# HGRN2 chunk scores in blocks of 64 tokens instead of 32, with a seventh masked level

## The chip, the cores and the metric

The kernel runs on one core of a Trainium2 chip. The metric is device time in microseconds (us) for one execution: the median of three executions is 2924.04 us (2918.29 to 2924.26).

## What is computed

The reference is one inference step of a decoder of two layers. Every layer projects 2064 prompt tokens (16 learned tokens and 2048 of the prompt) and 8 sample tokens by one combined matrix. Four mixers work on the columns of the product: HGRN2, gated DeltaNet, Mamba-2 SSD and retention, with four heads of 64 channels each. One output projection closes the layer. The change is inside HGRN2, whose decay is a vector: each key channel has its own decay at each token.

```python
def chunk_vector_decay(S, xs):
    q, k, v, g = xs
    G = jnp.cumsum(g, axis=2)
    causal = jnp.tril(jnp.ones((c, c), bool))
    diff = G[:, :, :, None, :] - G[:, :, None, :, :]
    decay = masked_exp(diff, causal[:, :, None])
    scores = jnp.einsum('bhik,bhjk,bhijk->bhij', q, k, decay)
    o = (jnp.einsum('bhij,bhjv->bhiv', scores, v)
         + jnp.einsum('bhik,bhkv->bhiv', q * jnp.exp(G), S))
    ...
```

A score of query i with key j needs the product of the decays between j and i in every channel, so the scores of a chunk are not one plain matrix product.

## The kernel before

The prompt is cut into a first tile (32 token rows for the 16 learned tokens and padding, with the 8 samples behind them) and 16 chunks of 128 tokens. Eight blocks of two chunks each (the first block has the small tile too) are the unit of the dense projections. A layer runs its mixers in turn: SSD (mixC), the dense part of gated DeltaNet (denseB and prepB), HGRN2 (mixA), retention (mixD), then the output projection. The serial walk over the gated DeltaNet states (walkB) is emitted in small parts, by hook(), among the work of the other mixers, above all in mixA. Dense products are made in three exact parts (lines 473 to 475 and 483 to 485) of 256 columns each.

mixA (from line 701) takes a block: dense products for q, f (the decay), kk, v and z, and then, for a group of two chunks (in the first block also a group of the small tile alone), the scores by levels. Level 0 (mask hm0) takes the diagonal: products of q and kk as they are. Then q is multiplied by its own token's decay and the loop at line 766 runs over h = 1, 2, 4, ... 64. At level h a pair counts if key and query lie in the left and right half of the same stretch of 2h tokens. Behind each level's products, right halves of q are multiplied by the left half's whole decay and left halves of kk by the right half's (lines 778 to 783), so that at the next level a plain product of q and kk is the decayed score again.

For levels 0 and h = 1 to 16 scores(32, 0) (line 736) multiplies blocks of 32 keys by the 32 queries of the same tokens: for a chunk 4 blocks x 2 pairs of heads x 2 heads of a pair = 16 products, each on 64 rows (a head's channels) and 32 columns of the TensorE array; the two heads lie in the two halves of the rows, the four blocks in the four quarters of the columns. merge (line 751) brings the level into the tile sm (`aS`, 128 x 256 for a group): level 0 by multiplying with its mask, the others by a predicated copy under the level's mask. At h = 32 and 64 scores(h, h) multiplies only the left half's keys by the right half's queries, and ScalarE copies the result directly into the chunk's full triangle (s128, tile `sq`; line 773). At the end GpSimd copies sm's four diagonal blocks into the triangle, eight copies a chunk (lines 804 to 807), and four products with v make the output (line 809).

All scores go through one PSUM buffer of two banks, pair() (line 199, one buffer). sm comes from w1 (tag W1, four buffers of 1 KB a partition, also used by `low` and `akt`); the running decay products aT come from w2 (tag W2, four buffers of 2 KB, also used by prepB for bR, bdc and others; line 215). Inputs are 32-bit floats, and each product of lines 745, 795 and so on shows in the trace as two matmul records, each with a weight load.

The order of instructions on each engine is not written out: a planner (the scheduler of the tile framework, line 1773) lays out a simulated timeline by priority and free buffers when the kernel is built, and each engine then runs its list in that order. What is emitted inside early() goes ahead in priority; inorder() fixes the order on chosen engines.

Of the kernel before, what the change touches and what calls it, by code (L numbers as in the profile page):

```python
# [33 lines left out]
def make_consts(nch):  # L34
    f = np.float32
# [22 lines left out]
    for n, h in enumerate((0, 1, 2, 4, 8, 16)):  # L58
        j = (p % 32)[:, None]
        if h == 0:  # L60
            parts[f"hm{n}"] = j == i32
        else:
            parts[f"hm{n}"] = (j // (2 * h) == i32 // (2 * h)) & (j % (2 * h) < h) & (i32 % (2 * h) >= h)
# [29 lines left out]
def body(tc, ctx, a, o, nch, depth, blks, off):  # L93
# [105 lines left out]
    def pair():  # L199
        """a bank per head half: row tiles of the array may not share a bank"""  # L200
# [44 lines left out]
    # ---------------------------------------------------------------- constants  # L245
# [15 lines left out]
    def fill():  # L261
# [6 lines left out]
        tt(strict, C("u32c"), C("hm0"), ALU.subtract)  # L268
# [5 lines left out]
    # block-diagonal states (two heads a tile), in turns  # L274
# [4 lines left out]
    # full triangles (upper halves written), in turns; outside of their use: norm weights, retention's decay  # L279
# [8 lines left out]
    def next_state(L, m, pu, decay):  # L288
        """S = decay * S + update, block-diagonal"""
# [25 lines left out]
    # ---------------------------------------------------------------- helpers  # L315
# [4 lines left out]
    def power(dst, src, k=0):  # L320
        """src ** -0.5 (k=0) or 0.5 (k=1)"""
# [23 lines left out]
    def rms_scale(hx, R):  # L345
        """1 / rms of the rows"""
# [6 lines left out]
    # ---------------------------------------------------------------- per layer parameters  # L353
    def load_layer(l):
# [38 lines left out]
        # forget gate bounds: softmax of the logits over the depth axis, cumulative  # L393
# [34 lines left out]
    # ---------------------------------------------------------------- dense pieces  # L428
# [66 lines left out]
    def xprep(L, t, hx, keep=False):  # L495
        """normalised rows of a token tile -> channel-major, in two exact parts, to DRAM or to the block's tiles"""
# [32 lines left out]
    def rowtile(b, nm):  # L529
        """token-major rows of 256 columns by tile"""  # L530
# [6 lines left out]
    def small(L, b, raw):  # L537
        """decays and step sizes from the narrow columns of a block's tiles"""
# [31 lines left out]
        # cumulative sums: ssd over the chunk, gdn over blocks of 32  # L570
# [15 lines left out]
    def group_scale(osrc, R, groups, eps):  # L586
        """rows scaled by 1 / rms of each group, in SBUF; eps: number or [R, groups]"""
# [26 lines left out]
    def finish(t, mi, osrc, R, eps, w, z, b=None):  # L614
        """group norm of the mixer rows; returns what takes them to channel-major, gate z [128, 2, R], and to DRAM"""
# [27 lines left out]
    # decode: partitions hold (head half, key), free (sample, pair, value)  # L643
# [12 lines left out]
    def dec_bcast(rows8):  # L656
        """[8, 256] rows -> [128 (hh k), (b p), 64]"""
# [8 lines left out]
    def pb(x, cols=None):  # L666
        """[128, 2, 8] channel-major sample columns -> [128, 8, 2, 64] broadcast over values"""
# [8 lines left out]
    def dec_sum(src, lhs, m):  # L676
        """sum over the key partitions"""
# [18 lines left out]
    # ---------------------------------------------------------------- HGRN2  # L696
# [4 lines left out]
    def mixA(L, W, b):  # L701
# [26 lines left out]
        for c0, Lc, tl in groups:  # L728
# [1057 lines left out]
```

## Time and profile before

| | |
|---|---|
| median of three executions | 2924.04 us (2918.29 to 2924.26) |
| span of the profiled execution | 2924.2 us |
| TensorE matmul busy | 2811.0 us (96%) |
| TensorE weight load busy | 2631.0 us (90%) |
| VectorE / ScalarE / GpSimd busy | 58% / 35% / 36% |
| HGRN2 stage with the walk beside it, layer 1 and layer 2 | about 650 to 1010 us, 2090 to 2500 us |

The span of the profiled execution lies within the three times, so nothing to speak of lies around it. PE is the matmul side of TensorE, PEld its weight loads, DVE is VectorE, ACT ScalarE, POOL GpSimd, SP the engine that issues most DMAs. Matmuls are pipelined: a record's duration is longer than the distance to the next record's start, so what a burst of matmuls costs is read from its first start to the start of what follows. Some records are missing from a trace.

### The profile page before, as it was taken

What the parts mean: (1) busy time and instruction counts of PE and PEld (TensorE: products, weight loads), DVE (VectorE), ACT (ScalarE), POOL (GpSimd) and SP (SyncE); (2) the same over time, 40 slices, a digit from 0 to 9 for tenths busy, and PEclk for the clock granted to TensorE, in tenths of its full rate; (3) what the DMA queues carried; (4) which work ended last, traced back from release to release, by engine and by line L of the source; (5) the groups of instructions that cost most, each with busy time, mean ns of one, the idle gap of its engine ahead of it and who ended that gap; (6) DMA issues with size and microseconds to landing.
All of it is one profiled execution on the core that took longest, in us unless ns stands there. A gap on an engine that the chain in (4) does not pass through costs nothing.

```text
span 2924.2 us, 76217 instructions
## 1 busy us (share of the span) xinstructions
PE 2811.0 (96%) x31196; PEld 2631.0 (90%) x31196; DVE 1694.9 (58%) x4822; ACT 1010.7 (35%) x2547; POOL 1045.4 (36%) x2000
## 2 busy tenths in 40 slices
PE   6989999999999999999999999899999999999998
PEld 6889898988888899999999999888988888999998
DVE  6777765646566745364456767565556657445433
ACT  5545522333333412232244454133333333222221
POOL 4453555665232211110033543745742222112000
PEclk9999999999999999999999999999999999999999
DMA  7243364462231432247762433645432222331433
GB/s 181 68 151 118 127 163 122 133 188 76 63 112 60 129 95 88 74 128 212 215 204 93 127 106 103 152 128 152 139 101 69 78 99 83 96 116 63 134 131 109
DMA packets 391332, 349.92 MB, mean 120 GB/s; under 512 B 144312, under 2 KB 361904, under 8 KB 380744
## 3 DMA queue, kind: packets, MB, share of 16 engines
q1 hardware_dynamic: 387464, 335.96, 37.5%
q0 software_dynamic: 3520, 9.09, 1.5%
q8 instruction: 247, 4.05, 0.6%
q14 instruction: 101, 0.83, 0.1%
HBM read 247.06 MB, written 98.10 MB: 118 GB/s over the span
## 4 chain that ended last, share of the span: by engine, by line
PE 84%; DVE 6%; DMA 4%; POOL 3%; ACT 2%; issue 2%; SPq 0%; POOLq 0%; ACTq 0%; DVEq 0%
PE pd L473 10%; PE pd L474 10%; PE pd L483 10%; PE pd L484 10%; PE pd L475 10%; PE pd L485 10%; PE tr L235 7%; PE sc L235 5%; PE wo L235 5%; PE o L235 3%; DMA wr<-in_w_in_dram 1%; PE tr L611 1%; PE tr L507 1%; DVE hx L502 1%; POOL bR L1110 1%
## 5 line engine op out<-in xcount | busy, mean ns | idle before, releaser
L473 PE MATMUL pd<-xh,wh 128*128 128x256 f32 (+1 forms) x2816 | 832.1, 296 | 12.6 <-DVE hB L901 3.3
L474 PE MATMUL pd<-xl,wh 128*128 128x256 f32 (+1 forms) x2816 | 817.9, 290 | 0.0
L475 PE MATMUL pd<-xh,wl 128*128 128x256 f32 (+1 forms) x2816 | 814.1, 289 | 0.0
L483 PE MATMUL pd<-wh,xh 128*128 128x256 f32 (+3 forms) x2448 | 702.0, 287 | 6.4 <-DVE sraw L1342 4.6
L484 PE MATMUL pd<-wl,xh 128*128 128x256 f32 (+3 forms) x2448 | 700.8, 286 | 2.5 <-POOL wl L450 2.5
L485 PE MATMUL pd<-wh,xl 128*128 128x256 f32 (+3 forms) x2448 | 698.0, 285 | 0.2
L473 PEld LDWEIGHTS pd<-xh,wh 128*128 128x128 f32 x2816 | 543.9, 193 | 37.2 <-issue 16.8
L474 PEld LDWEIGHTS pd<-xl,wh 128*128 128x128 f32 x2816 | 543.8, 193 | 9.1 <-issue 6.6
L475 PEld LDWEIGHTS pd<-xh,wl 128*128 128x128 f32 x2816 | 543.6, 193 | 4.1 <-issue 2.6
L483 PEld LDWEIGHTS pd<-wh,xh 128*128 128x128 f32 (+1 forms) x2448 | 455.7, 186 | 12.6 <-issue 5.4
L484 PEld LDWEIGHTS pd<-wl,xh 128*128 128x128 f32 (+1 forms) x2448 | 455.8, 186 | 9.0 <-issue 3.4
L485 PEld LDWEIGHTS pd<-wh,xl 128*128 128x128 f32 (+1 forms) x2448 | 455.7, 186 | 4.4 <-issue 2.1
L304 DVE TENSOR_TENSOR sbd<-low,tr 64x128 f32<-64x128 f32 x384 | 109.0, 284 | 131.8 <-PE tr L235 113.4
L600 POOL TENSOR_SCALAR fm<-fm 128x4 f32<-128x4 f32 (+3 forms) x102 | 23.7, 233 | 419.2 <-DVE fm L597 393.1
L1613 DVE TENSOR_TENSOR hx<-hx,pd 128x256 f32<-128x256 f32 (+1 forms) x136 | 57.1, 420 | 175.5 <-PE pd L485 175.2
L327 POOL TENSOR_TENSOR fm<-fm,expo 128x4 f32<-128x4 f32 (+3 forms) x136 | 129.3, 951 | 49.0 <-DVE fm L602 38.7
L331 POOL TENSOR_SCALAR rm<-rm 128x1 f32<-128x1 f32 (+1 forms) x51 | 13.7, 269 | 367.2 <-ACT junk L349 366.3
L520 ACT ACTIVATE th<-pd 128x256 f32<-128x256 f32 (+2 forms) x162 | 62.3, 384 | 231.8 <-PE pd L475 194.9
L235 PEld LDWEIGHTS sc<-aq,ak 64*32 64x32 f32 (+1 forms) x7008 | 97.0, 108 | 39.7 <-issue 16.9
L235 PE MATMUL sc<-aq,ak 64*32 64x32 f32 (+1 forms) x7008 | 129.1, 200 | 2.5 <-ACT sq L773 2.0
L1110 POOL TENSOR_TENSOR bR<-bR,bW 128x120 f32<-128x120 f32 (+14 forms) x300 | 119.6, 399 | 21.6
L1109 POOL TENSOR_TENSOR bW<-bU,bR 128x120 f32<-128x120 f32 (+14 forms) x300 | 112.6, 375 | 36.4 <-DMA bR<-bscr 15.4
(519 smaller groups left out, 4989.0 us busy)
## 6 DMA issues: line engine op xcount, KB each, us to landing
xh<-xh SPq DMA_DIRECT2D x56, 1024.0 KB
xl<-xl SPq DMA_DIRECT2D x56, 1024.0 KB
wr<-in_w_in_dram SPq DMA_DIRECT2D x64, 512.0 KB
hx<-in_x_prompt_dram SPq DMA_DIRECT2D x32, 512.0 KB
y<-y SPq DMA_DIRECT2D x128, 128.0 KB
yf<-y SPq DMA_DIRECT2D x32, 512.0 KB
bld<-qkv SPq DMA_DIRECT2D x32, 384.0 KB
xh<-xh SPq DMA_DIRECT2D x8, 1184.0 KB
```

The source lines that it names most:

```text
L235: T.matmul(out, l, r, start=start, stop=stop, skip_group_check=True)
L304: tt(new[rr, :, hh], low[rr, :, hh], pv, ALU.add)
L327: G.tensor_tensor(dst, src, e.broadcast_to(list(src.shape)), ALU.pow)
L473: T.matmul(ps, hi[:, d], b.xh[:, d, 0:b.n], start=(d == 0), stop=False)
L474: T.matmul(ps, hi[:, d], b.xl[:, d, 0:b.n], start=False, stop=False)
L475: T.matmul(ps, lo[:, d], b.xh[:, d, 0:b.n], start=False, stop=(d == 7))
L483: T.matmul(ps[0:R, 0:n], xh[:, d], hi, start=(d == 0), stop=False)
L484: T.matmul(ps[0:R, 0:n], xh[:, d], lo, start=False, stop=False)
L485: T.matmul(ps[0:R, 0:n], xl[:, d], hi, start=False, stop=(d == 7))
L520: act(th[0:R, 0:n], ps, AF.Tanh, scale=0.5)
L1109: f(wv, bcm(U_[0:2 * nu, j, j + 1:32], 1, m), bcl(R_[0:2 * nu, 0:m, j], 31 - j), ALU.mult)
L1110: f(R_[0:2 * nu, 0:m, j + 1:32], R_[0:2 * nu, 0:m, j + 1:32], wv, ALU.subtract)
```

## The change

The blocks on which a level's products are made become 64 keys by 64 queries (H = 64; 32 for the small tile): for a chunk 2 blocks x 2 x 2 = 8 products, each on 64 rows and 64 columns of the array, so that the two heads and the two blocks fill its four quarters. h = 32 becomes a level like the others (mask hm6, `copy_predicated`) and no longer goes through ScalarE; h = 64 stays (across()). The loop over the blocks stands inside the one over the head pairs. sm doubles to 128 x 512 for a group and moves from w1 to w2. GpSimd copies two diagonal blocks of 64 a chunk, four copies instead of eight. The masks hm0 to hm6 are 64 columns wide, and a separate identity e32 takes the place of hm0 where gated DeltaNet used it; the constant table grows from 756 to 1044 columns. The other lines of the diff take out comments.

```diff
-    for n, h in enumerate((0, 1, 2, 4, 8, 16)):
-        j = (p % 32)[:, None]
+    i64 = np.arange(64)
+    for n, h in enumerate((0, 1, 2, 4, 8, 16, 32)):
+        j = (p % 64)[:, None]
...
+    parts["e32"] = (p % 32)[:, None] == i32
...
-            def scores(h, w):
-                pv = pair()[:, :, 0:ncn * 2 * h].rearrange("j x (c p i) -> j x c p i", c=ncn, p=2)
+            H = min(64, Lc)
+
+            def scores():
+                pv = pair()[:, :, 0:ncn * 2 * H].rearrange("j x (c p i) -> j x c p i", c=ncn, p=2)
                 for c in range(ncn):
-                    for j0 in range(0, Lc, h + w):
-                        cc = c0 + Lc * c + j0
-                        for p in range(2):
+                    for p in range(2):
+                        for j0 in range(0, Lc, H):
+                            cc = c0 + Lc * c + j0
                             for hh in range(2):
                                 rr = slice(64 * hh, 64 * hh + 64)
-                                mm(pv[j0:j0 + h, hh, c, p], kk[rr, p, cc:cc + h], q[rr, p, cc + w:cc + w + h],
+                                mm(pv[j0:j0 + H, hh, c, p], kk[rr, p, cc:cc + H], q[rr, p, cc:cc + H],
                                    start=(c == 0 and p == 0), stop=True)
                 return pv
+            def across():
+                pv = pair()[:, :, 0:ncn * 2 * 64].rearrange("j x (c p i) -> j x c p i", c=ncn, p=2)
...
+                            mm(pv[0:64, hh, c, p], kk[rr, p, cc:cc + 64], q[rr, p, cc + 64:cc + 128],
+                               start=(c == 0 and p == 0), stop=True)
...
-            sm = w1([128, 2, 2, 2, 32], "aS")
+            sm = w2([128, 2, 2 * ncn, H], "aS")
...
-                if h < 32:
-                    merge(k, scores(32, 0))
+                if h < 64:
+                    merge(k, scores())
                 else:
-                    pv = scores(h, h)
+                    pv = across()
                     for c in range(ncn):
-                        for j0 in range(0, 128, 2 * h):
-                            S.copy(s128[(L.tai + c) % 2][j0:j0 + h, :, j0 + h:j0 + 2 * h].rearrange(
-                                "j (p x) i -> j x p i", p=2), pv[j0:j0 + h, :, c])
+                        S.copy(s128[(L.tai + c) % 2][0:64, :, 64:128].rearrange("j (p x) i -> j x p i", p=2), pv[0:64, :, c])
...
-                    for bb in range(4):
-                        r = slice(32 * bb, 32 * bb + 32)
+                    for bb in range(2):
+                        r = slice(64 * bb, 64 * bb + 64)
                         for x in range(2):
-                            gcopy(sf[r, x::2, r], sm[r, x, c])
+                            gcopy(sf[r, x::2, r], sm[r, x, 2 * c:2 * c + 2])
```

## Rows read from the trace of the kernel before

**Rows 1.** Page, part 1: busy us, share of the span and instructions by engine
```profile
PE 2811.0 (96%) x31196; PEld 2631.0 (90%) x31196; DVE 1694.9 (58%) x4822; ACT 1010.7 (35%) x2547; POOL 1045.4 (36%) x2000
```

**Rows 2.** Windows, HGRN2 stage of both layers: stretch and length, then busy by engine, clock
```profile
754.40:1010.00 255.60, 252.31 (x4042) 222.21 (x4040) 161.00 (x500) 98.71 (x270) 73.20 (x182) 0.99 0.28 90
2150.00:2480.00 330.00, 324.02 (x5330) 285.68 (x5329) 211.56 (x661) 120.84 (x334) 93.57 (x234) 0.99 0.27 84
```

**Rows 3.** Waits of PE, 640 to 1010 us: total us, times, longest
```profile
PE o L235 <- DVE sbd L304: 1.1, 1, 1.1
```

**Rows 4.** Instructions on the scores' PSUM tile: ns min/median/max, first and last start, forms
```profile
L235 PE MATMUL sc<-aq,ak x7008: 186/193/267, 650.7 to 2485.1; 64*32 64x32 f32 x187, 64*64 64x64 f32 x8
...
L773 ACT COPY sq<-sc x96: 237/256/368, 699.3 to 2485.6; 32x128 f32<-32x128 f32 x64, 64x256 f32<-64x256 f32 x32
```

**Rows 5.** Windows of the scores' tile alone, one group: PE, PEld, DVE, ACT busy
```profile
709.50:753.70 44.20, 7.84 (x432) 5.79 (x432) 2.62 (x6) 1.64 (x6) 1.00 0.28 85
```

**Rows 6.** Timeline of PE: start us, us, instructions merged; single bursts and what follows
```profile
843.91 0.32 PE L235 MATMUL sc<-aq,ak 64*32 64x32 f32 x8
844.15 0.45 PE L235 MATMUL tr<-bwi,bkt 32*64 32x64 f32 x8
844.53 0.44 PE L235 MATMUL sc<-aq,ak 64*32 64x32 f32 x24
...
848.47 0.68 PE L235 MATMUL sc<-aq,ak 64*64 64x64 f32 x16
849.08 0.39 PE L473 MATMUL pd<-xh,wh 128*128 128x256 f32 x1
849.31 0.28 PE L474 MATMUL pd<-xl,wh 128*128 128x256 f32 x1
849.43 0.28 PE L475 MATMUL pd<-xh,wl 128*128 128x256 f32 x1
...
876.53 0.82 PE L235 MATMUL sc<-aq,ak 64*32 64x32 f32 x64
877.28 0.39 PE L474 MATMUL pd<-xl,wh 128*128 128x256 f32 x1
```

**Rows 7.** Same view as group 4: VectorE on the scores
```profile
L758 DVE COPY_PREDICATED aS<-cst,sc x90: 285/441/455, 654.8 to 2477.9; 128x256 f32<-128x256 uint32 x80, 32x128 f32<-32x128 uint32 x10
...
L1556 DVE TENSOR_TENSOR css<-sc,sq x34: 278/690/692, 1063.4 to 2728.3; 128x512 f32<-128x512 f32 x32, 32x128 f32<-32x128 f32 x2
L756 DVE TENSOR_TENSOR aS<-sc,cst x18: 272/416/426, 651.3 to 2454.6; 128x256 f32<-128x256 f32 x16, 32x128 f32<-32x128 f32 x2
```

**Rows 8.** Groups of POOL by form, 640 to 1010 us: busy, mean ns, idle before
```profile
L243 POOL COPY sq<-aS 32x64 f32<-32x64 f32 x112 | 26.8, 266 | 21.0 <-DVE aS L758 18.9
...
L243 POOL COPY bgx<-g 128x256 f32<-128x256 f32 x11 | 4.6, 417 | 39.6 <-DVE sbd L304 32.5 <-issue 7.1
```

**Rows 9.** Timeline of DVE: merges of successive levels of one group
```profile
773.19 0.45 DVE L758 COPY_PREDICATED aS<-cst,sc 128x256 f32<-128x256 uint32 x1
...
780.23 0.44 DVE L758 COPY_PREDICATED aS<-cst,sc 128x256 f32<-128x256 uint32 x1
```

**Rows 10.** Instructions on aT, aS and bR where the layer's HGRN2 stage begins
```profile
L784 DVE TENSOR_TENSOR aT<-af x3: 426/473/484, 638.8 to 669.2; 128x256 f32<-128x256 f32 x2, 128x32 f32<-128x32 f32 x1
...
L756 DVE TENSOR_TENSOR aS<-sc,cst x2: 273/348/423, 651.3 to 673.9; 32x128 f32<-32x128 f32 x1, 128x256 f32<-128x256 f32 x1
...
L1112 POOL DMA_DIRECT2D bscu<-bR x2: 827/858/888, 659.3 to 660.2; - x2
...
DMA to landing us min/median/max: 3.6/4.1/4.5
```

**Rows 11.** A drop of the clock: PE's timeline ahead of it, and its window
```profile
752.61 0.41 PE L813 MATMUL tr<-ident,ak 128*128 128x128 f32 x2 [1.05 <-DVE sbd L304]
...
754.00:758.00 4.00, 4.00 (x20) 3.78 (x19) 1.92 (x6) 1.08 (x4) 1.20 (x2) 0.50 0.06 19
```

**Rows 12.** Windows, start of the execution: clock, DMA share and GB/s stand last
```profile
0.00:100.00 100.00, 73.53 (x517) 68.62 (x518) 63.84 (x194) 49.87 (x121) 46.27 (x66) 0.97 0.60 151
```

More of the change, by code (lines that the diff above doesn't have):

```diff
@@ L57, in make_consts @@
     parts = {}
-    for n, h in enumerate((0, 1, 2, 4, 8, 16)):
-        j = (p % 32)[:, None]
+    i64 = np.arange(64)
+    for n, h in enumerate((0, 1, 2, 4, 8, 16, 32)):
+        j = (p % 64)[:, None]
         if h == 0:
-            parts[f"hm{n}"] = j == i32
+            parts[f"hm{n}"] = j == i64
         else:
-            parts[f"hm{n}"] = (j // (2 * h) == i32 // (2 * h)) & (j % (2 * h) < h) & (i32 % (2 * h) >= h)
+            parts[f"hm{n}"] = (j // (2 * h) == i64 // (2 * h)) & (j % (2 * h) < h) & (i64 % (2 * h) >= h)
+    parts["e32"] = (p % 32)[:, None] == i32
     same = blk[:, None] == blk
@@ L267, in fill @@
         V.tensor_copy(ibf, ident)
-        tt(strict, C("u32c"), C("hm0"), ALU.subtract)
+        tt(strict, C("u32c"), C("e32"), ALU.subtract)
         for x in (*sbd, tb, mb, hones):
@@ L734, in hv @@
                 return x[:, :, c0:c0 + n].rearrange("c p (n s h) -> c p n s h", s=2, h=h)
-            def scores(h, w):
-                pv = pair()[:, :, 0:ncn * 2 * h].rearrange("j x (c p i) -> j x c p i", c=ncn, p=2)
+            H = min(64, Lc)
+            def scores():
+                pv = pair()[:, :, 0:ncn * 2 * H].rearrange("j x (c p i) -> j x c p i", c=ncn, p=2)
                 for c in range(ncn):
-                    for j0 in range(0, Lc, h + w):
-                        cc = c0 + Lc * c + j0
-                        for p in range(2):
+                    for p in range(2):
+                        for j0 in range(0, Lc, H):
+                            cc = c0 + Lc * c + j0
                             for hh in range(2):
                                 rr = slice(64 * hh, 64 * hh + 64)
-                                mm(pv[j0:j0 + h, hh, c, p], kk[rr, p, cc:cc + h], q[rr, p, cc + w:cc + w + h],
+                                mm(pv[j0:j0 + H, hh, c, p], kk[rr, p, cc:cc + H], q[rr, p, cc:cc + H],
                                    start=(c == 0 and p == 0), stop=True)
                 return pv
-            sm = w1([128, 2, 2, 2, 32], "aS")
+            def across():
+                pv = pair()[:, :, 0:ncn * 2 * 64].rearrange("j x (c p i) -> j x c p i", c=ncn, p=2)
+                for c in range(ncn):
+                    cc = c0 + 128 * c
+                    for p in range(2):
+                        for hh in range(2):
+                            rr = slice(64 * hh, 64 * hh + 64)
+                            mm(pv[0:64, hh, c, p], kk[rr, p, cc:cc + 64], q[rr, p, cc + 64:cc + 128],
+                               start=(c == 0 and p == 0), stop=True)
+                return pv
+            sm = w2([128, 2, 2 * ncn, H], "aS")
             def merge(k, pv):
-                mk = C(f"hm{k}")[0:Lc]
-                so = sm[0:Lc, :, 0:ncn].rearrange("j x c p i -> j x (c p) i")
+                mk = C(f"hm{k}")[0:Lc, 0:H]
+                so = sm[0:Lc]
                 pvv = pv[0:Lc].rearrange("j x c p i -> j x (c p) i")
@@ L758, in merge @@
                     V.copy_predicated(so, bcm(bcm(mk.bitcast(U32), 1, 2 * ncn), 1, 2), pvv)
-            merge(0, scores(32, 0))
+            merge(0, scores())
             qg = q[:, :, c0:c0 + n]
@@ L798, in mixA @@
                     for h4 in range(4):
-                        mm(ov[0:32, 64 * h4:64 * h4 + 64], sm[0:32, h4 % 2, c, h4 // 2], v[t][0:32, 64 * h4:64 * h4 + 64],
+                        mm(ov[0:32, 64 * h4:64 * h4 + 64], sm[0:32, h4 % 2, h4 // 2], v[t][0:32, 64 * h4:64 * h4 + 64],
                            start=(h4 == 0), stop=True)
@@ L1078, in prepB @@
         dg = w2([128, 2, 2 * nchk, 32], "bdg")
-        tt(dg, pv[:, :, 0, 0:nchk].rearrange("j x t p i -> j x (t p) i"), bcm(bcm(C("hm0"), 1, 2 * nchk), 1, 2), ALU.mult)
+        tt(dg, pv[:, :, 0, 0:nchk].rearrange("j x t p i -> j x (t p) i"), bcm(bcm(C("e32"), 1, 2 * nchk), 1, 2), ALU.mult)
         V.tensor_reduce(sk[:, k0:nt].rearrange("j t (p x) -> j x (t p)", x=2), dg, AX.X, ALU.add)
@@ L1142, in keysB @@
             r = slice(32 * bb, 32 * bb + 32)
-            gtt(tb[r, :, r], X.tc[r], bcm(C("hm0")[r], 1, 4), ALU.subtract)
+            gtt(tb[r, :, r], X.tc[r], bcm(C("e32")[r], 1, 4), ALU.subtract)
         ps = ptile(ptr, "tr")
```

## The prediction

> **What bounds the kernel now.** I read three views, from the whole to the stage. The page's first part has PE busy for 96% of the span and VectorE, next to it, for 58% [rows 1]. That is an average, so I went to the windows of the stage that changes: in HGRN2's stretches PE is busy for 252.3 of 255.6 us and for 324.0 of 330, at a granted clock of 0.99, and VectorE for 161.0 and 211.6, which is 63 to 64% [rows 2]. The waits of PE confirm it: the longest single one between 640 and 1010 us is 1.1 us [rows 3]. While scores and walk proceed level by level, the planner fills PE with dense matmuls of the next block, so PE has something queued nearly always. What the stage costs is thus the sum of PE's work, and a change there is worth what it takes from or adds to PE's list, unless it makes PE wait.
>
> A busy PE isn't a full PE. So the next view is the timeline of single bursts of score matmuls, and how they stand to what follows [rows 6]. A whole level of a group, 64 records of 64x32, starts at 876.53 and the next matmul at 877.28: 0.75 us. Eight records of the same form take 0.24 us (843.91 to 844.15), so each further record adds 0.51 / 56 = 9 ns. The eight tiles of the array that such a burst uses get only eight records each.
>
> **What a level will cost on PE.** No level of 64x64 on four quarters is in the trace, but its parts are. At h = 64, 16 records of 64x64 go to two tiles (the two heads' rows, the same half of the columns), eight records a tile: 848.47 to 849.08, 0.61 us. In the walk eight records with 64 moving columns go from the same 32 rows to the two halves of the columns, four a tile: 844.15 to 844.53, 0.38 us [rows 6]. Row halves and column halves both run side by side, then, and both fit one line: 0.15 us plus 0.058 us for every record on a tile. The new level has 32 records on four tiles, eight a tile: 0.15 + 8 x 0.058 = 0.61 us. Its 32 records at the 9 ns above would be issued within 0.15 + 0.29 us, so issue isn't the limit any more; the columns are. A level goes from 0.75 to 0.61 us.
>
> **Per group.** One group with all its records in the trace has PE busy with score matmuls for 7.84 us, 432 records [rows 5]. In busy time a burst counts some 0.07 us more than to the next start (0.82 against 0.75, 0.68 against 0.61) [rows 6]. Undivided, the group would be 6 levels x 0.82 + about 0.45 for h = 32 (half as many records; the burst of 24 shows 0.44) + 0.68 for h = 64 = 6.05 us. The other 1.8 us are bursts that the planner cut up to let walk and norm work in. Each cut pays the fixed 0.15 + 0.07 = 0.22 us once more, so there are about 8 cuts in a group.
>
> After: 7 levels x 0.68 + 0.68 = 5.44 us undivided. If all 8 cuts stay, 5.44 + 1.8 = 7.24: a gain of 0.6 us a group, 9.6 us for the 16 groups of both layers. A cut that goes away spares its 0.22 us and also a slow restart of the dense work: after a burst the second dense matmul comes 0.23 us behind the first (849.08 to 849.31) where the next follows in 0.12 [rows 6], so 0.33 us in all. With no cuts the gain is 0.6 + 8 x 0.33 = 3.2 us a group, 52 us in all. How many cuts remain is the planner's doing and shows in no row. Cuts come when other work becomes ready within a burst, and a level now is half as many instructions to cut into; but the planner's own estimate of 64 columns may be as long as that of twice 32. I take a third of the cuts gone: 0.6 + 2.7 x 0.33 = 1.5 us a group, **24 us in 16 groups**. The small tile's two groups keep blocks of 32 and stay as they are.
>
> **VectorE.** A merge over 512 elements in place of 256: the predicated copy takes 285 ns at 128 and 441 at 256, so 156 for 128 more and about 0.75 us at 512; the masked multiply goes from 416 ns to the 690 of retention's multiply of the same shape [rows 7]. Five predicated copies gain 0.31 each, the sixth is new with 0.75, the multiply gains 0.27: 2.6 us a group, 41 us in 16. In a group's 44 us [rows 5] that lifts VectorE from 64 to 70%: not a bound. It lies beside PE's work as long as the chain of levels has slack. Two successive merges of a group stand 7 us apart (773.19, 780.23) [rows 9], where a level's own chain, a burst (0.75) and five VectorE steps (441 ns and four of about the same or less), is under 3 us. The 0.31 us are hidden there. Behind the longer merge on VectorE's queue stand the walk's additions, and PE's waits on these are the ones that the list of waits shows [rows 3].
>
> **ScalarE and GpSimd.** 64 copies of h = 32 go, about 0.25 us each [rows 4]: 16 us off an engine at 35%, worth nothing. GpSimd's eight copies a chunk of 32x64 (266 ns) [rows 8] become four of 64x128. Their price lies between 266 and the 417 ns of a copy of 256 elements; I take 0.33. So 16 copies and 4.3 us become 8 and 2.6. But they start one level later, since the last merge is now that of h = 32, and before the output products only h = 64 is left to hide them. If that cover is gone, PE pays up to 2.6 us a group, 42 us in all; with 40 us of other dense work in a group I expect little.
>
> For the longer merges, the later copies and whatever the new order leaves of waits I give back 6 us, between nothing (all hidden) and 42 (every group waits for its copies). The clock can move either way: a drop to half speed (0.50 from 754 to 758) comes after light work and a wait of 1.05 us [rows 11], and such drops are few in the stage's windows (0.99) [rows 2].
>
> **Constants.** The table grows from 756 to 1044 columns: 147 KB more, at the 151 GB/s of the first 100 us [rows 12] 1 us of transfer, ahead of weight loads on the same queue. 0 to 1 us; I take 1.
>
> **Sum.** 2924.2 (the span of the profiled execution, within the three times) - 24 + 6 + 1 = **2907 us**.
>
> **A rule against it.** The Trainium skill, "TensorEngine Tiling (Array Packing)", Overview, section Theoretical Speedup, gives a dimension of 32 or less up to four times the throughput and one of 64 or less up to twice; by it blocks of 32 should be kept. By the 9 ns a record of [rows 6] the eight tiles aren't what a level waits for, so here the trace speaks against the rule.
>
> **Rivals.** (1) *The array is the limit and fewer tiles lose.* If row halves and column halves together don't run side by side as each pair does alone, sixteen records share a tile's time: 0.15 + 16 x 0.058 = 1.08 us, 0.33 more than before for six levels and about 0.7 for h = 32: 2.7 us a group, 43 us, and 2967. If they do, but a burst's 0.75 us came from its operands rather than its number of records, the doubled columns add 8 x 0.029 (half of 0.058) = 0.23 us a level, 7 levels and 16 groups: 26 us, 2950. Against both: the walk's 0.38 and the 0.61 at h = 64 [rows 6]. Chance 0.06.
>
> (2) *Slower by buffers*: sm moves into w2's four buffers. Where HGRN2 begins, three aT are written from 638.8 on, and the third only at 669.2; bR of an earlier part holds a buffer until its DMA out, issued at 660.2, has landed 4.5 us later; the next bR is in use too [rows 10]. The first sm is written at 651.3. If the planner gives the buffers to aT and bR first, the small tile's group waits until 664.7: 13.4 us. It decides as soon as PE has no more dense work to put there, since blocks ahead need buffers of their own; in both layers 27 us, less the gain of 18: 2933. For it: the third aT, which came right after that release. Against it: sm is asked for ahead of aT in the program, and early aT work isn't needed early. Chance 0.10.
>
> (3) *No visible change*: all cuts stay (-10) and the later copies and longer merges cost PE half a microsecond a group (+8): 2922. For it: the planner simulates, and doesn't see that bursts overlap on tiles. Chance 0.16.
>
> (4) *Nearly all cuts vanish*: the gain of 52 less the 7 given back, 2879. Chance 0.08. The forecast has 0.60.
>
> **How the numbers follow.** About 0.2%, 6 us, is what a measurement of this kernel tells from no change. Forecast and (4) are faster: 0.68. (3) is the same: 0.16. (1) and (2) are slower: 0.16. The range of 8 in 10 reaches from (4) to just above (2): 2879 to 2935.
>
> **What would show it.** In the new trace: (7 x 32 + 16) x 16 + 96 = 3936 score records in place of the 7008 [rows 4]; an undivided burst of 32 records of 64x64 with the next start 0.61 us on (1.08 would be rival 1); PE's busy time on the scores 6 to 7 us a group; predicated copies of 0.75 us; copies of 64x128 near 0.33; HGRN2's stretches shorter by about 10 us a layer, with PE still at 98%. The forecast is wrong if PE waits for `sq` or for `aS` by more than 0.5 us a group, if the first merge of the small tile moves behind 664 us, or if bursts come in smaller pieces than before.

## The result and the profile after

The changed kernel takes 2950.9 us (median of four executions, 2938.15 to 2956.08); the kernel before took 2924.15 us beside it. The ratio is 1.0093, 95% interval 1.0066 to 1.012: slower by 0.9%, where 2907 was forecast, and outside the range.

The first lines are the page's part 1, and two windows like those of [rows 2]:

```profile
PE 2820.6 (96%) x28124; PEld 2633.9 (89%) x28124; DVE 1727.5 (59%) x4838; ACT 993.7 (34%) x2483; POOL 1021.0 (35%) x1872
```

```profile
760.00:1010.00 250.00, 238.84 (x2914) 208.45 (x2915) 163.04 (x489) 85.78 (x234) 61.64 (x134) 0.98 0.26 82
2150.00:2500.00 350.00, 336.10 (x4130) 292.76 (x4129) 231.58 (x692) 119.04 (x324) 91.87 (x206) 0.97 0.26 81
```

Over the whole program PE's 96% is what it was [rows 1]. In the stage PE is now busy for 95.5 and 96.0% of the windows, where it was 98.7 and 98.2% [rows 2], and its clock fell from 0.99 to 0.98 and 0.97. The work on PE became no longer; PE stands, and runs slower. The groups of the two lists by line and form say what it stands for. Columns are busy us, mean ns of one, then the idle time just ahead of them and what ended it:

```profile
L237 PE MATMUL sc<-aq,ak 64*64 64x64 f32 (+1 forms) x3936 | 125.6, 232 | 16.6 <-DVE aS L774 5.6 <-DVE aq L778 5.5 <-DVE aT L798 4.3
...
L774 DVE COPY_PREDICATED aS<-cst,sc 128x512 f32<-128x512 uint32 x96 | 70.5, 735 | 2.3 <-PE sc L237 1.0
...
L772 DVE TENSOR_TENSOR aS<-sc,cst 128x512 f32<-128x512 f32 x16 | 11.0, 689 | 6.3 <-PE sc L237 6.2
...
L245 POOL COPY sq<-aS 64x128 f32<-64x128 f32 x128 | 37.6, 320 | 40.1 <-DVE aS L774 37.2
```

The score matmuls have 16.6 us of idle time ahead of them, nearly all of it ended by VectorE's steps of the levels (15.4 by aS, aq and aT). In the kernel before it was 2.5, and none of it was put down to these three:

```profile
L235 PE MATMUL sc<-aq,ak 64*32 64x32 f32 (+1 forms) x7008 | 129.1, 200 | 2.5 <-ACT sq L773 2.0 <-DVE ak L779 0.4
```

Between 640 and 1085 us the waits of PE, whose longest single one was 1.1 us [rows 3], begin with these:

```profile
PE sc L237 <- DVE aq L778: 3.9, 3, 2.2
PE sc L237 <- DVE aT L798: 3.8, 3, 1.8
PE sc L237 <- DVE aS L774: 3.7, 5, 1.1
PE tr L237 <- ACT akt L829: 2.4, 3, 1.4
```

Where these waits come from is seen at the beginning of a group. This is the timeline around level 0 and level 1 of the group that begins at 1022.56 (start, us, engine, line, what):

```profile
1022.56 0.69 PE L237 MATMUL sc<-aq,ak 64*64 64x64 f32 x32
...
1023.19 0.65 PE L237 MATMUL wo<-sbd,bnq 128*64 128x128 f32 x4
...
1023.45 1.21 DVE L452 TENSOR_TENSOR wl<-wr,wh 128x1024 fp32r<-128x1024 f32 x1
...
1024.58 0.68 DVE L772 TENSOR_TENSOR aS<-sc,cst 128x512 f32<-128x512 f32 x1
1025.19 0.68 DVE L778 TENSOR_TENSOR aq<-aq,af 128x512 f32<-128x512 f32 x1
...
1026.01 0.69 PE L237 MATMUL sc<-aq,ak 64*64 64x64 f32 x32 [2.18 <-DVE aq L778]
...
1027.81 0.73 DVE L774 COPY_PREDICATED aS<-cst,sc 128x512 f32<-128x512 uint32 x1
...
1029.33 0.92 PE L237 MATMUL sc<-aq,ak 64*64 64x64 f32 x24 [1.81 <-DVE aT L798]
```

PE's list has four matmul records of the walk (two products) between level 0 and level 1, and then level 1, which needs the merge of level 0 and the multiplication of q. VectorE does a weight's low part first (1.21 us), then these two (0.68 each). PE stands for 2.18 us, and at level 2 for 1.81. Its list is fixed when the kernel is built, so the dense matmuls that stand behind level 1 can't go ahead. And the clock falls behind such places (in these windows the clock stands third from the end, ahead of DMA share and GB/s):

```profile
1018.00:1028.00 10.00, 7.34 (x120) 5.95 (x118) 7.50 (x17) 5.71 (x15) 0.73 (x2) 1.00 0.53 190
1028.00:1035.00 7.00, 5.67 (x57) 4.41 (x58) 6.18 (x21) 1.57 (x5) 0.73 (x2) 0.51 0.21 75
...
690.00:704.00 14.00, 12.57 (x216) 10.67 (x208) 8.23 (x27) 3.24 (x10) 9.65 (x27) 0.99 0.66 214
704.00:721.00 17.00, 17.00 (x146) 14.87 (x143) 11.12 (x34) 5.15 (x16) 4.53 (x11) 0.50 0.01 2
```

In the first of these stretches PE stands for 2.66 us of 10, and then runs at 1.2 GHz (0.51) for 7 us; in the third it stands for 1.43 us of 14, and then runs at that level (0.50) for 17 us. In both layers' stages together, as they are bounded in the next paragraph, stretches at half clock sum to 68 us, before to 34.

**The account.** I measured the stage in each layer from the last matmul of gated DeltaNet's preparation (sc<-bk) to retention's first (sc<-dqk) and laid PE's time out from start to start. The stages grew from 468.1 to 486.7 and from 469.8 to 479.5 us, 28.3 in all. Of that, idle time is +17.0 (26.5 to 43.5) and time lost to half clock +17.1 (15.1 to 32.2; half of PE's busy time in these stretches). The score bursts, put at full clock, gave 2.7 (108.9 to 106.2). The rest gave 3. Elsewhere in the program 5 us went the other way. So two questions stood: why did the bursts bring 3 us and not 24, and what makes PE stand?

### The profile page after: what moved, and what is told of

Its sections match the earlier page's. It is cut to its first block, busy times and chain, and to the rows that moved or that the text cites. A ratio compares the mean times of both kernels' runs of the same rounds, so it can differ in the third digit from the quotient of the medians.

```text
span 2947.7 us, 69824 instructions
## 1 busy us (share of the span) xinstructions
PE 2820.6 (96%) x28124; PEld 2633.9 (89%) x28124; DVE 1727.5 (59%) x4838; ACT 993.7 (34%) x2483; POOL 1021.0 (35%) x1872
## 5 line engine op out<-in xcount | busy, mean ns | idle before, releaser
L602 POOL TENSOR_SCALAR fm<-fm 128x4 f32<-128x4 f32 (+3 forms) x102 | 20.7, 203 | 411.3 <-DVE fm L599 362.5
L237 PE MATMUL sc<-aq,ak 64*64 64x64 f32 (+1 forms) x3936 | 125.6, 232 | 16.6 <-DVE aS L774 5.6
L237 PEld LDWEIGHTS sc<-aq,ak 64*64 64x64 f32 (+1 forms) x3936 | 92.5, 137 | 51.1 <-issue 23.0
L523 DVE SCALAR_TENSOR_TENSOR z<-th,pd 128x256 f32<-128x256 f32 (+1 forms) x96 | 39.6, 423 | 151.1 <-ACT th L522 150.7
```

The lines of the kernel that those rows point to most:

```text
L237: T.matmul(out, l, r, start=start, stop=stop, skip_group_check=True)
```

## Why the bursts brought so little

The bursts themselves did what was forecast. A whole level of 32 records of 64x64 in the kernel after, then a level cut in two by the walk:

```profile
777.85 0.69 PE L237 MATMUL sc<-aq,ak 64*64 64x64 f32 x32
778.48 0.39 PE L477 MATMUL pd<-xh,wl 128*128 128x256 f32 x1
...
781.94 0.44 PE L237 MATMUL sc<-aq,ak 64*64 64x64 f32 x10
782.32 0.65 PE L237 MATMUL wo<-sbd,bnq 128*64 128x128 f32 x4
782.90 0.57 PE L237 MATMUL sc<-aq,ak 64*64 64x64 f32 x22
783.40 0.39 PE L475 MATMUL pd<-xh,wh 128*128 128x256 f32 x1
```

A cut level of the kernel before, for comparison:

```profile
731.49 0.39 PE L235 MATMUL sc<-aq,ak 64*32 64x32 f32 x30
731.81 0.45 PE L235 MATMUL tr<-bwi,bkt 32*64 32x64 f32 x8
...
732.77 0.46 PE L235 MATMUL sc<-aq,ak 64*32 64x32 f32 x34
733.16 0.39 PE L483 MATMUL pd<-wh,xh 128*128 128x256 f32 x1
```

The whole level takes 0.63 us to the next start (0.61 was forecast). Cut, it takes 0.38 + 0.50 = 0.88: the cut costs 0.25. Before, the halves take 0.32 + 0.39 = 0.71, no more than the 0.75 of a whole level [rows 6]: that cut costs nothing, and one of 8 and 56 records (0.245 and 0.680 at 737.66 and 727.12) costs 0.18. Over all: 281 bursts before, of which 140 would be there uncut, so 141 cuts; uncut they would take 6 x 0.747 + 0.37 + 0.61 a group and 2.9 for the small tiles, 90 us of the 108.9, which leaves 0.13 a cut. After: 236 bursts, 96 cuts, uncut 7 x 0.625 + 0.61 a group and 2.9, 83 of 106.2, which leaves 0.24 a cut. A third of the cuts is gone, as forecast, but each one that stays costs 0.11 more, some 10 us, and that eats what the shorter levels bring.

## The experiments

Two theories at the start. *Chain*: merges of 0.73 us in place of 0.44 lengthen the levels' chain on VectorE, PE meets it at the next level, and waits and half clock follow. *Buffers*: sm in w2 takes one of its four buffers from aT and the others, and the levels come late for that. All ratios are to the kernel before, run beside each.

**Half of each merge left out.** Short merges on the kernel after: behind level 0, the scores in the right half of the columns are left out.

```diff
+                    w = H if Lc == 32 else 32
-                    V.copy_predicated(so, bcm(bcm(mk.bitcast(U32), 1, 2 * ncn), 1, 2), pvv)
+                    V.copy_predicated(so[:, :, :, 0:w], bcm(bcm(mk[:, 0:w].bitcast(U32), 1, 2 * ncn), 1, 2), pvv[:, :, :, 0:w])
```

> The changed kernel, but every merge behind level 0 writes only the left 32 of the 64 columns (the rest of the diagonal blocks' scores is left out), so a merge costs 0.44 us as before and not 0.73; products, buffers and copies stay as changed. Theory 'chain' (longer merges on VectorE make PE wait at the groups' ends, and the waits lower the clock): most of the loss goes, 2918 to 2930 us, PE's idle time in the two stages falls from 43 us to under 32. Theory 'buffers' (sm in w2 makes aT late): unchanged, 2945 to 2955. Theory 'products' (the 64-column products and the order that the planner makes of them): unchanged too.

1.0038 (1.0023 to 1.0052). Idle in the stages falls from 43.5 to 33.9 us, a little less than *chain* expected (under 32), and the loss to half clock from 32.2 to 20.7. More than half of the slowdown goes in this run, but not all.

**One more buffer for w2.**

```diff
-    NW1, NW2, NBLK, NF4, NE, NF, NBK = 4, 4, 9, 5, 4, 4, 11
+    NW1, NW2, NBLK, NF4, NE, NF, NBK = 3, 5, 9, 5, 4, 4, 10
```

> The changed kernel with five w2 buffers in place of four, paid for with one w1 buffer (3 for 4; sm has left w1) and one BK buffer of the walk (10 for 11). Theory 'buffers': 2920 to 2932, the waits of PE on aT go. Theory 'chain' and theory 'products': 2943 to 2957.

1.0032 (1.0018 to 1.0045). That looks like *buffers*, but the row of the score matmuls shows that what the theory explains isn't gone: 17.4 us of idle ahead of them, 42.8 in the stages, as in the kernel after. Of the 24 us between the two profiled spans 13 lie outside the stages (1968 us in place of 1981); why this layout is faster there was not looked into.

**Each merge twice, blocks of 32.**

```diff
...
+                    for _ in range(2):
-                    V.copy_predicated(so, bcm(bcm(mk.bitcast(U32), 1, 2 * ncn), 1, 2), pvv)
+                        V.copy_predicated(so, bcm(bcm(mk.bitcast(U32), 1, 2 * ncn), 1, 2), pvv)
```

> The kernel before, each merge made twice: 0.42 + 5 x 0.44 = 2.6 us more of VectorE a group, as much as the change adds, and nothing else is changed. Theory 'chain': 2940 to 2955 with more idle time of PE at the groups' ends. Theory 'buffers' and theory 'products': 2920 to 2930.

1.008 (1.0065 to 1.0095), with idle 41.4 and half clock 35.9, nearly those of the kernel after. The waits are others, though, at the walk:

```profile
PE wo L235 <- DVE sbd L304: 4.1, 3, 1.5
PE tr L235 <- DVE sbd L304: 2.7, 4, 0.9
```

**sm in w2, blocks of 32.**

```diff
-            sm = w1([128, 2, 2, 2, 32], "aS")
+            sm = w2([128, 2, 2, 2, 32], "aS")
```

> The kernel before with sm in w2 in place of w1, nothing else. Theory 'buffers': 2938 to 2955. Theory 'chain' and theory 'products': 2920 to 2930.

0.9991 (0.9975 to 1.0007): no change. It leaves one mark: idle ahead of the score matmuls is 8.4 us in place of 2.5, in many small pieces.

**h = 32 through ScalarE again, blocks of 64.** The 32x32 products, the copies by ScalarE and GpSimd's eight copies a chunk, of four blocks of 32, as in the kernel before; the other levels as after.

```diff
-                if h < 64:
+                if h < 32 or Lc == 32:
                     merge(k, scores())
+                elif h == 32:
+                    pv = pair()[:, :, 0:ncn * 2 * 32].rearrange("j x (c p i) -> j x c p i", c=ncn, p=2)
...
```

> The changed kernel with the seventh level undone: h = 32 goes through products of 32x32 and ScalarE into the triangle as before, GpSimd copies four blocks of 32 a chunk as before; blocks of 64 stay for level 0 and h = 1 to 16. VectorE then has 1.8 us more a group than before, where the change has 2.6. Theory 'chain': about a third of the loss goes, 1.004 to 1.008 of the kernel before. Theory 'products': 1.008 to 1.011, as the change.

1.0102 (1.0083 to 1.0121). Undoing the seventh level gives nothing back, though its bursts are 7 us shorter (98.7).

**Merges over the right-half columns only.** At level h only the right halves of 2h columns can count, so a merge needs only half of the columns.

```diff
-                    V.copy_predicated(so, bcm(bcm(mk.bitcast(U32), 1, 2 * ncn), 1, 2), pvv)
+                    hh_ = 2 ** (k - 1)
+                    so, pvv = (x.rearrange("j c (n s h) -> j c n s h", s=2, h=hh_)[:, :, :, 1] for x in (so, pvv))
+                    mk = mk.bitcast(U32).rearrange("j (n s h) -> j n s h", s=2, h=hh_)[:, :, 1]
+                    V.copy_predicated(so, bcm(mk, 1, 4 * ncn), pvv)
...
```

On the kernel after:

> The changed kernel whole, but a merge behind level 0 writes only the columns that its mask can touch (the right halves, 32 of 64), in one instruction over 256 elements; the scores' buffer is laid out with 128 columns between pairs for this. Merges at 0.44 us in place of 0.73, the same result. Theory 'chain': as the run with the left half of the columns only, 1.002 to 1.006. Theory 'products': 1.008 to 1.011.

1.0056 (1.0039 to 1.0072). With h = 32 through ScalarE as well:

> Both of these: h = 32 on ScalarE as before and merges over half the columns. VectorE has 0.3 us a group more than before (level 0's multiply), PE still makes blocks of 64. Theory 'chain': back at the kernel before, 0.997 to 1.002. Theory 'products' (64-column products or the order planned around them cost by themselves): 1.003 to 1.010.

1.0056 (1.0038 to 1.0075). On the kernel before:

> The kernel before, blocks of 32, with merges over half the columns (128 elements, 0.29 us in place of 0.44): 0.8 us less of VectorE a group. Theory 'chain': a little faster than before, 0.994 to 0.999, with PE's idle time and the slow clock in the stage at or below those of before. Theory 'products': no change, 0.999 to 1.001.

0.9957 (0.994 to 0.9973), 2904.41 us against 2915.86: faster than both kernels. So shorter merges help on either side, but blocks of 64 with short merges still lose 0.5% to the kernel before. Of what is left, the row of a_cols shows the place; the same idle as after, hardly less of it:

```profile
L237 PE MATMUL sc<-aq,ak 64*64 64x64 f32 (+1 forms) x3936 | 123.2, 229 | 13.9 <-DVE aq L781 5.6 <-DVE ak L796 4.4 <-DVE aS L777 2.2
```

**Only the products in blocks of 64; sm back in w1; another order.** The first takes the kernel before and makes only the products 64x64, for level 0 and h = 1 to 16; it merges only half of them. The second takes the half-width merges of a_cols and puts sm into w1 as two tiles of a chunk each. The third takes one buffer from the walk, so that the planner lays out the same work in another order.

```diff
+            def scores64():
...
+                return pv[:, :, :, :, 0:32]
...
+            sc0 = (lambda: scores(32, 0)) if Lc == 32 else scores64
...
```

> The kernel before, in which only the products of level 0 and of h = 1 to 16 are made as 64x64 blocks (32 records a level in place of 64); the merges read the left 32 of the 64 columns, 256 elements as before, sm stays in w1, h = 32 and 64 and GpSimd's copies stay as they were. The scores of the lower blocks of 32 in each block of 64 are left out by this. Theory 'products' (the 0.5% that stays in the kernel after when its merges are short comes from the 64x64 products and the order planned for them): ratio to before 1.003 to 1.007, PE waits of 12 to 18 us ahead of score bursts in the two stages (before 2.5). Theory 'together' (the products alone cost nothing; the rest comes from sm's doubled tile in w2 with them): ratio 0.997 to 1.001, waits under 6 us. Prediction's own burst sum: 24 us less, ratio 0.992.

```diff
-            sm = w2([128, 2, 2 * ncn, H], "aS")
+            sms = [w1([128, 2, 2, H], "aS") for _ in range(ncn)]
...
```

> The kernel after with merges over the right-half columns only, as in a_cols, and sm split by chunk into two tiles of 1 KB in w1, so that w2's buffers are left to aT and the walk as before; each level's merge becomes two instructions (about 2 x 0.30 us in place of 0.44). Theory 'buffers with 64-blocks': ratio 0.998 to 1.001 in place of a_cols's 1.0056. Theory 'products': 1.004 to 1.008, the two merges costing a little on top.

```diff
-    NW1, NW2, NBLK, NF4, NE, NF, NBK = 4, 4, 9, 5, 4, 4, 11
+    NW1, NW2, NBLK, NF4, NE, NF, NBK = 4, 4, 9, 5, 4, 4, 10
```

> The kernel before with one buffer less for the walk's operands (10 in place of 11) and no other edit: the planner lays out another order of the same instructions. It measures how far a new order alone moves the time. If the ratio lies within 0.998 to 1.002, a difference of 0.4% is more than a new order's chance; if it is off by 0.4% or more, the 0.5% that stays in a_cols can be such a chance.

0.999 (0.9974 to 1.0007), 0.9989 (0.9973 to 1.0004) and 0.9998 (0.9977 to 1.0019). The products cost nothing, and don't bring what the sum said either (score bursts 98.9 in place of 108.9, no visible change in time). With sm in w1 the loss is gone, although a group's merges then take 5.0 us, as long as in the kernel after:

```profile
L237 PE MATMUL sc<-aq,ak 64*64 64x64 f32 (+1 forms) x3936 | 123.7, 228 | 1.9 <-DVE aS L777 1.7 <-DVE ak L800 0.2
```

**A buffer of its own for sm.** If it were a lack of buffers, this must help.

```diff
-            sm = w2([128, 2, 2 * ncn, H], "aS")
+            sm = k1.tile([128, 2, 2 * ncn, H], F32, tag="AS", name="aS")
...
-    NW1, NW2, NBLK, NF4, NE, NF, NBK = 4, 4, 9, 5, 4, 4, 11
+    NW1, NW2, NBLK, NF4, NE, NF, NBK = 3, 4, 9, 5, 4, 4, 10
```

With whole merges:

> The kernel after with the merges as they are (512 elements, 0.73 us) and one edit: sm has one 2 KB buffer of its own instead of one of w2's four, so that w2 is left to aT, bR and the others as in the kernel before (the room comes from w1's fourth buffer, which sm no longer uses, and from one of the walk's eleven). Theory 'buffer alone' (the merges' time costs nothing when the order is not pressed together): ratio 0.997 to 1.001 and under 5 us of PE waits ahead of score bursts. Theory 'both' (longer merges cost about 0.4 to 0.5% by themselves, sm in w2 as much again): 1.003 to 1.006, waits under 8 us. Theory 'merges alone': 1.008 to 1.010, as the kernel after, waits 15 us or more.

With half-width merges:

> a_own1 with the merges over the right-half columns only (256 elements, 0.44 us a level), that is a_cols without sm in w2. Theories 'buffer alone' and 'both': 0.994 to 0.999, near the 0.9957 of blocks of 32 with half-width merges, since the scores' bursts themselves cost no more than before; PE waits ahead of score bursts under 5 us. Theory 'merges alone': 1.003 to 1.006, as a_cols.

1.0072 (1.0046 to 1.0097) and 1.0072 (1.0048 to 1.0096). None of the three expectations holds. *Buffers* falls, and the waits are where they were (the row is that of whole merges):

```profile
L237 PE MATMUL sc<-aq,ak 64*64 64x64 f32 (+1 forms) x3936 | 131.1, 235 | 16.3 <-DVE aq L778 7.8 <-DVE ak L793 6.2 <-DVE aS L774 1.5
```

What the kernels that lose have in common is found in TensorE's instruction list: the number of matmul instructions between a group's level 0 and level 1. In the kernel before it is 25 to 52 in each of the 16 groups. In the kernel after it is 2 to 10 in 11 of them. So it is in every kernel up to here whose sm isn't in w1 (9 to 12 groups), and in none whose sm is. In w1 sm shares four buffers with `low` and `akt`, and a group's first merge is due only when one of them is free: on the median it starts 2.5 us behind the start of its burst's last record before, 0.3 us after and 0.6 us with a_own1. With room for sm at once, the planner sets level 1 right behind level 0, and the few matmuls between don't cover VectorE's two steps and what else is in its queue. That makes a third theory, *order*.

**The order held apart, sm still in w2.** Two masks are copied into a tile of w1 and read from there. That ties the group's first merge to a free buffer of w1 again.

```diff
             sm = w2([128, 2, 2 * ncn, H], "aS")
+            hold = w1([128, 2, 2, 64], "aH")
+            gcopy(hold[0:Lc, 0, 0, 0:H], C("hm0")[0:Lc, 0:H])
+            kl = 5 if Lc == 32 else 6
+            gcopy(hold[0:Lc, 0, 1, 0:H], C(f"hm{kl}")[0:Lc, 0:H])
...
-                mk = C(f"hm{k}")[0:Lc, 0:H]
+                mk = hold[0:Lc, 0, int(k > 0), 0:H] if k in (0, kl) else C(f"hm{k}")[0:Lc, 0:H]
```

> The kernel after with whole merges and sm in w2, and one addition: at the start of a group GpSimd copies the masks of level 0 and of the last merge (64 columns each) into a tile of w1, and these two merges read them there. No other arithmetic changes; a group's first merge now comes due when a buffer of w1 is free, as in the kernel before, and TensorE's list has 33 to 120 matmul instructions between level 0 and level 1 of a group where the kernel after has 2 to 10 in 11 of its 16 groups. Theory 'order' (what a_cols and the runs with an own buffer still lose comes from level 1 standing too close behind level 0 on PE's list): PE waits ahead of score bursts under 6 us (after 16.6), ratio to before 1.001 to 1.005, the rest being the longer merges. Theory 'order alone' (the merges cost nothing then): 0.997 to 1.001. Theory 'buffers' (w2's fourth buffer is what is missing): 1.008 to 1.010, nothing changed.

With half-width merges:

> a_hold with the merges over the right-half columns only (0.44 us), that is a_cols with the order held apart: 27 to 118 matmul instructions between level 0 and level 1 (a_cols: as the kernel after). Theory 'order': 0.994 to 0.999 in place of 1.0056, waits under 5 us. Theory 'buffers': 1.004 to 1.007, as a_cols.

1.0029 (1.0012 to 1.0045) and 1.0027 (1.0011 to 1.0044). The first has the arithmetic, the merges and w2's buffers of the kernel after (GpSimd's two mask copies a group are added), and two thirds of the slowdown are gone. Its row and its two windows:

```profile
L237 PE MATMUL sc<-aq,ak 64*64 64x64 f32 (+1 forms) x3936 | 122.2, 229 | 3.8 <-DVE aS L778 3.6
```

```profile
760.00:1010.00 250.00, 243.97 (x3027) 212.93 (x3026) 167.94 (x492) 91.36 (x242) 67.10 (x147) 1.00 0.29 91
2150.00:2500.00 350.00, 343.58 (x4157) 301.08 (x4155) 226.92 (x675) 116.50 (x314) 90.70 (x200) 0.97 0.25 80
```

Idle ahead of the scores is 3.8 us in place of 16.6, and PE is busy for 97.6 and 98.2% of the windows. By level, 12.5 of the 16.6 us stand ahead of h = 1, 2 and 4 (5.5, 4.8 and 2.2), and in a_hold none. So the waits go with the order. Short merges add nothing to that, against *order*'s expectation for them.

The clock doesn't follow. In the second window it is 0.97, as in the kernel after, and in this profiled execution (the slowest of a_hold's ten) the stages lose 33.8 us to half clock, after 32.2. The profiled span is 18 us shorter than that of the kernel after; 9 of these lie in the stages and 9 outside. So the trace shows that the hold takes the waits away, and the ratio that the time falls; how much of the time fell because of the waits is not shown.

**What the merges' length costs by itself.** a_w1two with whole merges (6.1 us a group), and the doubled and the half-width merges of the kernel before in another order.

```diff
...
-                        V.copy_predicated(so, bcm(mk, 1, 4), pvv)
+                        V.copy_predicated(so, bcm(bcm(mk.bitcast(U32), 1, 2), 1, 2), pvv)
```

> a_w1two with whole merges: sm in two tiles of 1 KB in w1, every level's merge two instructions of 256 elements (0.44 us each), 6.1 us of VectorE a group in place of a_w1two's 5.0 and the kernel before's 2.6. TensorE's list has 29 to 60 matmul instructions between level 0 and level 1 of a group. Theory 'the merges' length costs by itself': 1.005 to 1.009, as twice the merges on the kernel before. Theory 'order only' (length is covered as long as the levels stand apart): 0.998 to 1.002, as a_w1two.

> The kernel before with each merge made twice, as in b_merge2, laid out once more with one buffer less for the walk's operands (an edit that alone measured 0.9998). If 1.008 was the doubled merges' own price, it stays at 1.006 to 1.010. If it was the order that the planner happened to lay out, it can fall to 1.000 to 1.004.

> The kernel before with merges over the right-half columns, as in b_cols, laid out once more with one buffer less for the walk's operands. If 0.9957 was the price of the shorter merges, it stays at 0.993 to 0.998; if it was the order, it can return to 0.999 to 1.001.

1.0026 (1.0012 to 1.004), 1.0017 (0.9992 to 1.0042) and 0.9963 (0.9947 to 0.9978). Whole merges in w1 cost 0.4% over a_w1two, with one layout of each; with the hold they cost nothing. The gain of half-width merges on blocks of 32 stands in both orders. The 1.008 of the doubled merges doesn't: in another order it is 1.0017, so most of it belonged to that order. What I had taken for proof of *chain* was in good part one order's doing.

The table has all of it: the merges of a group on VectorE (from the durations), the groups of 16 with ten or fewer matmul instructions between level 0 and level 1, PE's idle time ahead of the score matmuls (the row shown above for some), and the ratio.

| kernel | merges, us | close groups | idle, us | ratio |
|---|---|---|---|---|
| before | 2.6 | 0 | 2.5 | 1 |
| half-width, two orders (b_cols, b_colsn) | 2.2 | 0 | 2.0, 1.8 | 0.9957, 0.9963 |
| another order (b_bk10) | 2.6 | 0 | 2.4 | 0.9998 |
| products of 64 (b_prod64) | 2.6 | 0 | 2.0 | 0.999 |
| in w1, half-width (a_w1two) | 5.0 | 0 | 1.9 | 0.9989 |
| held, half-width (a_holdc) | 3.9 | 0 | 2.3 | 1.0027 |
| held (a_hold) | 5.1 | 0 | 3.8 | 1.0029 |
| in w1, whole (a_w1full) | 6.1 | 0 | 3.4 | 1.0026 |
| doubled, two orders (b_merge2, b_merge2n) | 5.2 | 0 | 4.6, 5.0 | 1.008, 1.0017 |
| sm in w2, blocks of 32 (b_w2) | 2.6 | 12 | 8.4 | 0.9991 |
| half left out (a_half) | 3.3 | 12 | 11.7 | 1.0038 |
| half-width (a_cols) | 3.9 | 12 | 13.9 | 1.0056 |
| own buffer, half-width (a_own1cols) | 3.9 | 12 | 8.7 | 1.0072 |
| own buffer (a_own1) | 5.1 | 12 | 16.3 | 1.0072 |
| h = 32 by ScalarE, half-width (a_l6cols) | 3.4 | 12 | 18.7 | 1.0056 |
| h = 32 by ScalarE (a_l6act) | 4.4 | 12 | 19.1 | 1.0102 |
| w2 with five (a_w2x5) | 5.1 | 9 | 17.4 | 1.0032 |
| **after** | 5.1 | 11 | 16.6 | 1.0093 |

Levels that stand close cost nothing with merges of 0.44 us on blocks of 32, and 0.3 to 1.0% with longer chains on blocks of 64. Levels that stand apart bring every kernel with sm's merges to 1.003 or less, but for one order. Ahead of level 1 PE stands for 2.9 to 8.0 us in every kernel with close groups, and not at all in any other. How long it stands doesn't set the ratio: a_own1cols has 8.7 us ahead of the scores and 1.0072, a_w2x5 17.4 and 1.0032.

## Why the prediction was wrong

**Right.** 3936 score records; 0.63 us for a whole level; a third of the cuts gone; merges of 0.73 and 0.69 us; GpSimd's copies at 0.32, with one wait of 0.8 us for `sq` in the second layer, so their later start is covered; ScalarE's copies worth nothing. Rival (1) is refuted by the 0.63 (its two forms gave 1.08 and 0.98); that its second form's 2950 us is nearly the measured time is chance. So the trace goes on speaking against the Trainium skill's rule, "TensorEngine Tiling (Array Packing)", Overview, section Theoretical Speedup: four quarters served a level in 0.63 us, eight tiles in 0.75. Rival (2)'s mechanism is refuted as well: the first sm is written at 654.0 (651.3 before), with no 13 us wait.

**The step that failed first: "the 0.31 us are hidden there".** It rested on two merges 7 us apart [rows 9] and a chain under 3 us, and read the distance as slack that belongs to the kernel. It belonged to the order, and the change took the order away. I went through sm's move from w1 to w2 as a question of too few buffers (rival 2) and of nothing else. What w1 did was the opposite: its scarcity held back a group's first merge, and so kept 25 to 52 matmul instructions between two levels. a_hold shows this: the hold alone takes away the waits ahead of h = 1, 2 and 4 and brings 1.0093 to 1.0029. Where the levels stand apart the longer merges do stay hidden, in the kernel after too: ahead of h = 8 and 16, with 22 to 40 matmul instructions behind the level before, PE doesn't stand at all.

**The give-back of 6 us was mis-sized.** Waits came to 17 us in the stages, inside the bounds of 0 to 42, but they stood ahead of the scores and not of the copies. The criterion, that the forecast is wrong if PE waits for aS by over 0.5 us a group, named the right place: the waits ahead of the scores are 16.6 us, 1.0 a group. For aS alone, as it was worded, they are 5.6 us or 0.35 a group, so that to the letter it was not met.

**The clock was left without a price.** It "can move either way" [rows 11]; it took 17 us, in this execution as much as the waits. In a stage where PE is busy for 98% and drops follow waits of one or two us (1.05 before the drop of [rows 11], 2.18 at 1026), a forecast of waits needs a second term for the clock. Its size is no fixed share of the waits: against the kernel before, a_cols has 13.8 us more idle time in the stages and 2.6 us more lost to half clock, a_hold 3.6 and 18.7.

**The 24 us of the bursts were mis-sized**: 2.7, for the price of a cut, taken as the same 0.22 before and after, is 0.13 for bursts of 64x32 and 0.24 for those of 64x64. PE's busy time on the scores, forecast at 6 to 7 us a group, is 125.6 us in all or 7.9 a group (129.1 before).

Summed: -2.7 in place of -24, +34 in place of +6 for waits and clock, -3 and -5 that were nobody's term: +23.5, the difference between the two profiled spans (2924.2 and 2947.7).

**What stays open.** With the levels apart the kernel with blocks of 64 is still 0.3% above the kernel before (a_hold, a_w1full), and a_w1two is not. Whole merges could account for that in a_w1full, but a_holdc has shorter merges than a_w1two and still measures 1.0027. In all kernels with sm in w2 the fifth group of each layer also lies differently (96 to 132 matmul instructions between its first two levels). Whether that is the difference wasn't tried. The granted clock of all executions tells where the time goes: its mean is 0.983 in a_hold, a_holdc and a_w1full, 0.986 and 0.985 in the kernel before beside them, and 0.987 in a_w1two. Over a whole execution that makes 8.7, 8.1 and 6.2 us more lost to half clock (an estimate: time by the clock's missing share, idle time included), and on the mean they are 8.8, 8.5 and 7.3 us longer. So what is left is about the size of the clock's loss. What brings that loss wasn't followed up.

## What to carry to other kernels

In a stage where one engine is 98% busy, slack seen in a timeline belongs to the order that a planner laid out, not to the work: before counting on it, ask which buffer or wait keeps the steps apart and whether the change removes that. Moving a tile to a roomier pool is a change of order, and a wait on the busy engine costs its own length and can cost time at half clock besides, which is to be read from the trace: here the added loss was a fifth of the added idle time in a_cols and five times it in a_hold. A difference of half a per cent between two layouts is read as a cause only once a second layout of the same edit shows it too.

## What the runs showed of the hardware

A predicated copy of half of the columns was shorter only where its columns lay in runs of four or more. These are the merges of one group of b_cols, level 0 and then h = 1, 2 and 4, 128 elements each from the second on:

```profile
749.83 0.42 DVE L757 TENSOR_TENSOR aS<-sc,cst 128x256 f32<-128x256 f32 x1
...
755.18 0.45 DVE L762 COPY_PREDICATED aS<-cst,sc 128x128 f32<-128x128 uint32 x1 [0.46 <-PE sc L235]
...
761.28 0.43 DVE L762 COPY_PREDICATED aS<-cst,sc 128x128 f32<-128x128 uint32 x1
...
767.13 0.29 DVE L762 COPY_PREDICATED aS<-cst,sc 128x128 f32<-128x128 uint32 x1
```

Runs of one or two columns (h = 1, 2) take 0.45 and 0.43 us, as the whole 256 elements did (0.441) [rows 7]; from runs of four on it is 0.29. At twice the size (a_cols) it is the same: 0.73 for h = 1 and 2, 0.43 from h = 4.

Score records of 64x32 aren't issued evenly: bursts of 30 took 0.32 us and of 34 0.39, of 64 0.75. The 9 ns a record of the forecast were a mean over both parts, and the first half of a burst is cheaper than the second. That is why cutting one in two cost nothing.
